# Chained partial sums in two PSUM banks for the seven-product FFN pairs of an encoder layer

## The chip, the cores and the metric

One Trainium2 chip, one core of it. Times are microseconds of device time for one execution of the whole layer. TensorE (PE) multiplies matrices from SBUF into PSUM, VectorE (DVE) and ScalarE (ACT) work on tiles in SBUF and PSUM, GpSimd (POOL) does little here, and SyncE (SP) issues the DMAs. Each engine runs its own instructions in the order in which they were put into its queue when the program was built.

## The reference

One layer over x of 512 tokens by 1024 channels, all in float32:

```
x = LN1(alpha*x + 0.5 * (silu(x @ wg1) * (x @ wu1)) @ wd1)      # FFN 1, inner width 2816
h = x @ w_in ; sparse attention (8 heads) and a short gated convolution on parts of h
x = LN2(alpha*x + concat(attention, convolution) @ w_out)
x = LN3(alpha*x + 0.5 * (silu(x @ wg2) * (x @ wu2)) @ wd2)      # FFN 2, inner width 2816
x = x + sigmoid(x @ w_gate) * (p @ w_proj)
```

The change touches the two products x @ wg and x @ wu of both FFNs and nothing else.

## The kernel before

Every float32 operand of a matmul is split into a high and a low part (`split`, L110: an ACT cast writes the high part, a DVE subtraction the low one), and each product is made of three passes, high x high, high x low, low x high (`PASSES`, L59).

An FFN (`ffn`, L239) goes over 22 chunks of 128 inner channels in five groups of 4, 4, 4, 4 and 6. The first two chunks of an FFN are computed plainly (`plain`). The others go in pairs (`two`, L302): ten pairs in each FFN, twenty in all. A pair computes, for wg and for wu, a 256-channel by 1024 by 512-token product as two by two by two blocks with seven block products instead of eight (Strassen's scheme in Winograd's form). The token side (`Quarters`) keeps the four blocks B11, B21, B22 and the sums T1 to T4; the weight side (`weights`, L269) loads the two row blocks `r` (two DMAs from L274 for each matrix), and makes A11, A12, A22 and the sums S1 to S4, each split into high and low. One product (`prod`, L312) of the pair fills one PSUM bank of 128 x 512: 12 matmuls of 256 columns for wg in one half, 12 for wu in the other half.

After the seven products the partial sums are put together in SBUF (L333 to L342): one copy on ACT and seven additions on DVE, each of which reads one PSUM bank. P5 = S1T1 is read twice. `put_chunk` then makes silu(gate) * up of one 128-channel chunk (L329 on ACT, L330 on DVE) and splits it. The end of each group is the down-projection with wd, matmuls of 512 columns that are accumulated over the group's chunks. In the groups of four these go chunk by chunk with four banks; in the last group they go token block by token block, and each needs all six chunks.

PSUM has eight banks, which `bank("all")` hands out in turn. SBUF tiles are 38 pages of 4 KB per partition in a first-in first-out list (`page`, `free`, L86 to L94). `free` only says in program order which page the next `page` takes; at run time the new owner waits until the last instruction on the old tile is done. A pair before takes 26 pages beside the two of its hidden chunks, gives back raw blocks and plain sums inside `weights`, and everything else (L344) after its second chunk. The loads of a new pair go into such pages too, so a load on SP waits for its page, and later loads wait behind it.

The order on each engine is made by a planner when the program is built. It goes through the program in simulated time; of the instructions that are ready there it takes the one earliest in the program. `tc.high_priority(offset=n)` moves a block n positions ahead in this order. A pair's weight work has a head start of 25 positions (the first pair of FFN 1), 100 (the others of FFN 1), 400 (the first pair of FFN 2) or 50 (the others of FFN 2); the weight rows of the down-projection have 125 in FFN 1 and 0 in FFN 2. A product of a pair is 24 positions long. `WSTEPS` (L31) sets in which turns the two generators of `weights` are pulled.

Of the kernel before, what the change touches and what calls it, by code (L numbers as in the profile page):

```python
# [7 lines left out]
F32 = mybir.dt.float32  # L8
# [4 lines left out]
P = 128  # L13
# [14 lines left out]
REPL = -3.0e38  # L28

NPAGES = 38  # L30
WSTEPS = (1, 2, 1)  # L31
BANKS = ((0, 1), (4, 5), (6,), (7, 2, 3))
AHEAD = 25
AHEAD_N = 150
# [24 lines left out]
PASSES = ((0, 0), (0, 1), (1, 0))  # L59
# [4 lines left out]
def layer_kernel(ctx: ExitStack, tc: tile.TileContext, x, ln1_g, ln1_b, ffn1_wg, ffn1_wu, ffn1_wd, w_in,  # L64
# [21 lines left out]
    def page(shape, dt=F32R):  # L86
        i = free_pages.pop(0)
        t = sb.tile(shape, dt, tag=f"pg{i}", name=f"pg{i}_{count('pg')}")
        owner[id(t)] = (i, t)
        return t  # L90

    def free(*tiles):
        for t in tiles:
            free_pages.append(owner.pop(id(t))[0])  # L94
# [4 lines left out]
    def bank(group):  # L99
        g = GROUPS[group]  # L100
        return pp.tile([P, 512], F32, tag=f"bk{g[count('bank' + group) % len(g)]}", name=f"bk_{count('bank')}")
# [8 lines left out]
    def split(hi, lo, src):  # L110
        nc.scalar.copy(hi, src)  # L111
        nc.vector.tensor_sub(lo, src, hi.bitcast(F32))  # L112
# [126 lines left out]
    def ffn(X, wg, wu, wd, ln_g, ln_b, first, load_nat, groups, nplain, ahead, ahead_f, ahead_d):  # L239
# [26 lines left out]
            nc.vector.tensor_mul(hf, s_t, ps["u"])  # L266
            return put(hf)

        def weights(w, fc, ops, pages):  # L269

            r = []
            for c in (0, 4):
                r.append(page([P, 4, 2 * P], F32))
                nc.sync.dma_start(r[-1], rows(w[:, fc * P:(fc + 2) * P], c * P, 4))  # L274
            A11, A21, A12, A22 = (r[k][:, :, m * P:(m + 1) * P] for k in range(2) for m in range(2))
            a11 = page([P, 2, 4, P])
            split(a11[:, 0], a11[:, 1], A11)
            ops["A11"] = a11[:, 0], a11[:, 1]
            yield
            a2 = page([P, 4, 2 * P]), page([P, 4, 2 * P])  # L280
            split(*a2, r[1])
            ops["A12"], ops["A22"] = (tuple(z[:, :, m * P:(m + 1) * P] for z in a2) for m in range(2))
            yield
            s12, s34 = page([P, 2, 4, P], F32), page([P, 2, 4, P], F32)
            S1, S2, S3, S4 = s12[:, 0], s12[:, 1], s34[:, 0], s34[:, 1]
            nc.vector.tensor_add(S1, A21, A22)  # L286
            nc.vector.tensor_sub(S2, S1, A11)  # L287
            h12 = page([P, 2, 4, P]), page([P, 2, 4, P])
            split(*h12, s12)
            ops["S1"], ops["S2"] = (tuple(z[:, i] for z in h12) for i in range(2))  # L290
            yield
            nc.vector.tensor_sub(S3, A11, A21)  # L292
            nc.vector.tensor_sub(S4, A12, S2)  # L293
            free(*r, s12)
            h34 = page([P, 2, 4, P]), page([P, 2, 4, P])
            split(*h34, s34)
            free(s34)
            ops["S3"], ops["S4"] = (tuple(z[:, i] for z in h34) for i in range(2))
            pages += [a11, *a2, *h12, *h34]
            yield  # L300

        def two(fc, ah):  # L302

            W, pages = {nm: {} for nm, _ in mats}, []
            steps = [weights(w, fc, W[nm], pages) for nm, w in mats]
            with tc.high_priority(offset=ah):
                for n in WSTEPS:
                    for g in steps:
                        for _ in range(n):
                            next(g)  # L310

            def prod(a, b):  # L312

                ps = bank("all").rearrange("p (m n) -> p m n", m=2)
                for i, (nm, _) in enumerate(mats):
                    mm(ps[:, i], [((W[nm][a][0][:, c], W[nm][a][1][:, c]), (X.q[b][0][:, c], X.q[b][1][:, c])) for c in range(4)])
                return ps


            e = [page([P, 2, 2, 256], F32) for _ in range(2)]  # L320
            k = [page([P, 2, 2, 256], F32) for _ in range(2)]
            p1, u2, u3, u4 = k[0][:, 0], k[0][:, 1], k[1][:, 0], k[1][:, 1]
            h = []

            def put_chunk(m):
                hf = ring("hf", 2, [P, 512])
                h3 = hf.rearrange("p (a b) -> p a b", a=2)
                s_t = ring("a", 2, [P, 2, 256])
                nc.scalar.activation(s_t, e[m][:, :, 0], AF.Silu)  # L329
                nc.vector.tensor_mul(h3, s_t, e[m][:, :, 1])  # L330
                h.append(put(hf))

            nc.scalar.copy(p1, prod("A11", "B11"))  # L333
            nc.vector.tensor_add(e[0][:, 0], prod("A12", "B21"), p1)
            nc.vector.tensor_add(u2, prod("S2", "T2"), p1)
            p5 = prod("S1", "T1")
            nc.vector.tensor_add(u4, p5, u2)
            nc.vector.tensor_add(e[0][:, 1], prod("S4", "B22"), u4)  # L338
            put_chunk(0)
            nc.vector.tensor_add(u3, prod("S3", "T3"), u2)  # L340
            nc.vector.tensor_add(e[1][:, 1], p5, u3)
            nc.vector.tensor_add(e[1][:, 0], prod("A22", "T4"), u3)  # L342
            put_chunk(1)
            free(*pages, *e, *k)  # L344
            return h

        f0 = 0
# [449 lines left out]
```

## Time and profile before

| | |
|---|---|
| median of 3 runs | 1026.12 us (1024.97 to 1027.34) |
| profiled execution | 1026.09 us |
| its span, first to last instruction | 1024.0 us |
| mean granted TensorE clock | 0.998 of full speed |
| TensorE, VectorE, ScalarE busy | 98%, 80%, 43% of the span |

All rows below come from the profiled execution. Its time has 2.1 us around the span. Busy time of TensorE counts a matmul from its start to a modelled end, so neighbours overlap; the distance of two starts tells the rate.

### The profile page before, as it was taken

The numbers are of one execution on the slowest core, as the hardware profiler recorded it, in microseconds if no ns is written. First come the engines' busy times: TensorE is split into PE (matmuls) and PEld (weight loads), VectorE is DVE, ScalarE is ACT, GpSimd is POOL, SyncE is SP. The second block draws the span as 40 slices with busy tenths as digits, with TensorE's granted clock in tenths as the row PEclk, the third lists the DMA queues.
The fourth block names the chain that finished last, engine by engine and source line by source line (L and its number), as shares of the span: only waits on it lengthen the run. The fifth ranks groups of instructions, "written<-read, shape, count | busy, mean of one in ns | idle before, by whom it ended". The sixth has DMA issues, their size and how long they took to land.

```text
span 1024.0 us, 15507 instructions
## 1 busy us (share of the span) xinstructions
PE 1004.6 (98%) x6313; PEld 903.8 (88%) x6313; DVE 822.2 (80%) x1283; ACT 441.8 (43%) x621; POOL 25.0 (2%) x35
## 2 busy tenths in 40 slices
PE   8999999999999999999999999999999999999998
PEld 7989999898998878888878778989999898998787
DVE  7897868978697958999479988896868969689852
ACT  6444424433354235332576836443425324246221
POOL 1000000000000200000000011000000000000100
PEclk9999999999999999999999999999999999999999
DMA  9342324323335231424013223331424322227111
GB/s 311 122 123 83 109 98 131 97 83 107 100 119 185 69 92 42 128 58 124 20 42 104 83 65 101 124 124 39 127 83 144 103 79 87 83 85 265 52 41 51
DMA packets 99510, 104.57 MB, mean 102 GB/s; under 512 B 5872, under 2 KB 81904, under 8 KB 99440
## 3 DMA queue, kind: packets, MB, share of 16 engines
q1 hardware_dynamic: 99440, 103.60, 31.8%
q8 instruction: 49, 0.80, 0.3%
q14 instruction: 21, 0.17, 0.1%
HBM read 101.49 MB, written 2.10 MB: 101 GB/s over the span
## 4 chain that ended last, share of the span: by engine, by line
PE 89%; DMA 4%; DVE 3%; ACT 3%; issue 1%; POOLq 0%; SPq 0%; ACTq 0%
PE bk L132 86%; ACT pg L111 2%; DVE pg L112 1%; DMA pg<-in_ffn_wu_dram 1%; PE bk L506 1%; DMA pg<-in_w_in_dram 1%; DMA pg<-in_x_t_dram 1%; PE bk L507 1%; PE bk L704 1%; DMA pg<-in_ple_proj_w_dram 1%; DMA pg<-in_ffn_wd_dram 0%; PE bk L146 0%; ACT a L676 0%; DMA pg<-in_ple_gate_w_dram 0%; PE bk L692 0%
## 5 line engine op out<-in xcount | busy, mean ns | idle before, releaser
L132 PE MATMUL bk<-pg,pg 128*128 128x256 f32 (+1 forms) x2832 | 496.4, 333 | 4.4 <-ACT pg L111 1.8
L132 PEld LDWEIGHTS bk<-pg,pg 128*128 128x128 f32 x2832 | 427.6, 190 | 56.0 <-ACT pg L111 2.6
L111 ACT CAST pg<-pg 128x1024 fp32r<-128x1024 f32 (+1 forms) x267 | 260.0, 984 | 313.3 <-PE bk L132 78.4
L112 DVE TENSOR_TENSOR pg<-pg,pg 128x1024 fp32r<-128x1024 f32 (+1 forms) x267 | 300.6, 1139 | 40.6 <-ACT pg L111 35.5
L132 PE MATMUL bk<-xq,pg 128*128 128x256 f32 x2208 | 275.3, 284 | 4.6 <-DVE mv L158 1.5
L132 PEld LDWEIGHTS bk<-xq,pg 128*128 128x128 f32 x2208 | 270.6, 193 | 7.0 <-ACT pg L111 2.3
L132 PE MATMUL bk<-xT,pg 128*128 128x512 f32 (+2 forms) x600 | 133.0, 381 | 0.3 <-ACT xT L111 0.2
L132 PEld LDWEIGHTS bk<-xT,pg 128*128 128x128 f32 (+1 forms) x600 | 109.9, 186 | 21.5 <-ACT xT L111 0.5
L132 PE MATMUL bk<-pg,xT 128*128 128x512 f32 (+1 forms) x312 | 69.5, 374 | 1.3 <-DVE nat L385 1.3
L132 PEld LDWEIGHTS bk<-pg,xT 128*128 128x128 f32 x312 | 55.0, 188 | 11.4 <-ACT pg L111 1.8
L329 ACT ACTIVATE a<-pg 128x512 f32<-128x512 f32 x40 | 25.2, 629 | 71.7 <-DVE pg L338 66.1
L111 ACT CAST pg<-hf 128x512 fp32r<-128x512 f32 (+1 forms) x56 | 34.6, 618 | 35.2 <-DVE hf L330 19.6
L112 DVE TENSOR_TENSOR pg<-hf,pg 128x512 fp32r<-128x512 f32 (+1 forms) x56 | 38.3, 684 | 4.7 <-ACT pg L111 4.5
L399 DVE SCALAR_TENSOR_TENSOR nat<-bk,nat 128x512 f32<-128x512 f32 x64 | 40.4, 682 | 0.8 <-PE bk L132 0.7
L330 DVE TENSOR_TENSOR hf<-a,pg 128x512 f32<-128x512 f32 x40 | 27.5, 688 | 13.6 <-ACT a L329 13.5
L338 DVE TENSOR_TENSOR pg<-bk,pg 128x512 f32<-128x512 f32 x20 | 13.8, 692 | 29.9 <-PE bk L132 29.4
L160 POOL TENSOR_TENSOR mv<-mv,mhalf 128x1 f32<-128x1 f32 x12 | 17.8, 1480 | 627.0 <-DVE mv L159 627.0
L286 DVE TENSOR_TENSOR pg<-pg,pg 128x512 f32<-128x512 f32 x40 | 27.3, 686 | 5.7 <-DMA pg<-in_ffn_wg_dram 5.7
L292 DVE TENSOR_TENSOR pg<-pg 128x512 f32<-128x512 f32 x40 | 27.4, 686 | 2.9 <-PE bk L132 2.9
L112 DVE TENSOR_TENSOR pg<-bk,pg 128x512 fp32r<-128x512 f32 (+2 forms) x37 | 22.5, 626 | 8.5 <-ACT pg L111 8.1
L287 DVE TENSOR_TENSOR pg<-pg,pg 128x512 f32<-128x512 f32 x40 | 27.3, 685 | 0.0
L293 DVE TENSOR_TENSOR pg<-pg,pg 128x512 f32<-128x512 f32 x40 | 27.1, 686 | 0.1
(100 smaller groups left out, 612.7 us busy)
## 6 DMA issues: line engine op xcount, KB each, us to landing
pg<-in_ffn_wg_dram SPq DMA_DIRECT2D x44, 512.0 KB, 4.1
pg<-in_ffn_wu_dram SPq DMA_DIRECT2D x44, 512.0 KB, 4.7
pg<-in_ffn_wd_dram SPq DMA_DIRECT2D x44, 512.0 KB, 4.0
pg<-in_w_in_dram SPq DMA_DIRECT2D x28, 512.0 KB, 3.6
pg<-in_w_out_dram SPq DMA_DIRECT2D x8, 512.0 KB, 3.9
pg<-in_ple_gate_w_dram SPq DMA_DIRECT2D x8, 512.0 KB, 4.8
pg<-in_x_t_dram SPq DMA_DIRECT2D x4, 512.0 KB, 7.5
nat<-in_x_dram SPq DMA_DIRECT2D x4, 512.0 KB, 8.9
```

Source lines behind the costliest of these rows:

```text
L111: nc.scalar.copy(hi, src)
L112: nc.vector.tensor_sub(lo, src, hi.bitcast(F32))
L132: nc.tensor.matmul(ps, lhsT=st[a], rhs=mv[b], start=first and i == 0 and k == 0, stop=last and i == n - 1 and k == 2)
L160: nc.gpsimd.tensor_tensor(mv[:, 3:4], mv[:, 2:3], mhalf, op=ALU.pow)
L286: nc.vector.tensor_add(S1, A21, A22)
L287: nc.vector.tensor_sub(S2, S1, A11)
L292: nc.vector.tensor_sub(S3, A11, A21)
L293: nc.vector.tensor_sub(S4, A12, S2)
L329: nc.scalar.activation(s_t, e[m][:, :, 0], AF.Silu)
L330: nc.vector.tensor_mul(h3, s_t, e[m][:, :, 1])
L338: nc.vector.tensor_add(e[0][:, 1], prod("S4", "B22"), u4)
L399: nc.vector.scalar_tensor_tensor(dst, acc[t], CY, dst, op0=ALU.mult, op1=ALU.add)
```

## The change

The seven products are computed in the order A11B11, S1T1, S2T2, S4B22, S3T3, A12B21, A22T4. Two PSUM banks, x and y, are each used for several of them, and later products add to what stands there: x holds A11B11, then A11B11 + S2T2, then that plus S3T3, then that plus A22T4; y holds S1T1, then S1T1 + S4B22. A12B21 has a third bank. Between two products the running sum is copied out by ACT (four copies in all) or added by DVE to what is already in the page (three additions). Only the first matmul on a bank has `start` set.

In `weights` the split of the second row block (A12, A22) is the last step instead of the second, S4 is computed before S3, and the two matrices are pulled in turn, one step each. The pages of an operand go back to the list after the product that uses it last, the pages of the sums `e` after their chunk, and the two pages `k` are gone. The hidden chunk m = 0 follows A12B21, the sixth product; before, it followed the fifth.

```diff
--- before.py
+++ after.py
@@ -28,7 +28,6 @@
 REPL = -3.0e38
 
 NPAGES = 38
-WSTEPS = (1, 2, 1)
 BANKS = ((0, 1), (4, 5), (6,), (7, 2, 3))
 AHEAD = 25
 AHEAD_N = 150
@@ -266,7 +265,8 @@
             nc.vector.tensor_mul(hf, s_t, ps["u"])
             return put(hf)
 
-        def weights(w, fc, ops, pages):
+        def weights(w, fc, ops):
+
 
             r = []
             for c in (0, 4):
@@ -275,11 +275,7 @@
             A11, A21, A12, A22 = (r[k][:, :, m * P:(m + 1) * P] for k in range(2) for m in range(2))
             a11 = page([P, 2, 4, P])
             split(a11[:, 0], a11[:, 1], A11)
-            ops["A11"] = a11[:, 0], a11[:, 1]
-            yield
-            a2 = page([P, 4, 2 * P]), page([P, 4, 2 * P])
-            split(*a2, r[1])
-            ops["A12"], ops["A22"] = (tuple(z[:, :, m * P:(m + 1) * P] for z in a2) for m in range(2))
+            ops["A11"] = (a11[:, 0], a11[:, 1]), [a11]
             yield
             s12, s34 = page([P, 2, 4, P], F32), page([P, 2, 4, P], F32)
             S1, S2, S3, S4 = s12[:, 0], s12[:, 1], s34[:, 0], s34[:, 1]
@@ -288,38 +284,51 @@
             h12 = page([P, 2, 4, P]), page([P, 2, 4, P])
             split(*h12, s12)
             ops["S1"], ops["S2"] = (tuple(z[:, i] for z in h12) for i in range(2))
-            yield
+            ops["S1"], ops["S2"] = (ops["S1"], []), (ops["S2"], h12)
+            yield
+            nc.vector.tensor_sub(S4, A12, S2)
             nc.vector.tensor_sub(S3, A11, A21)
-            nc.vector.tensor_sub(S4, A12, S2)
-            free(*r, s12)
+            free(r[0], s12)
             h34 = page([P, 2, 4, P]), page([P, 2, 4, P])
             split(*h34, s34)
             free(s34)
             ops["S3"], ops["S4"] = (tuple(z[:, i] for z in h34) for i in range(2))
-            pages += [a11, *a2, *h12, *h34]
+            ops["S3"], ops["S4"] = (ops["S3"], h34), (ops["S4"], [])
+            yield
+            a2 = page([P, 4, 2 * P]), page([P, 4, 2 * P])
+            split(*a2, r[1])
+            free(r[1])
+            ops["A12"], ops["A22"] = (tuple(z[:, :, m * P:(m + 1) * P] for z in a2) for m in range(2))
+            ops["A12"], ops["A22"] = (ops["A12"], []), (ops["A22"], a2)
             yield
 
         def two(fc, ah):
 
-            W, pages = {nm: {} for nm, _ in mats}, []
-            steps = [weights(w, fc, W[nm], pages) for nm, w in mats]
+            W = {nm: {} for nm, _ in mats}
+            steps = [weights(w, fc, W[nm]) for nm, w in mats]
             with tc.high_priority(offset=ah):
-                for n in WSTEPS:
+                for _ in range(4):
                     for g in steps:
-                        for _ in range(n):
-                            next(g)
-
-            def prod(a, b):
-
-                ps = bank("all").rearrange("p (m n) -> p m n", m=2)
+                        next(g)
+
+            def bank2():
+                return bank("all").rearrange("p (m n) -> p m n", m=2)
+
+            def product(ps, a, b, first):
+
                 for i, (nm, _) in enumerate(mats):
-                    mm(ps[:, i], [((W[nm][a][0][:, c], W[nm][a][1][:, c]), (X.q[b][0][:, c], X.q[b][1][:, c])) for c in range(4)])
+                    w = W[nm][a][0]
+                    for c in range(4):
+                        for k, (x_, y_) in enumerate(PASSES):
+                            nc.tensor.matmul(ps[:, i], lhsT=w[x_][:, c], rhs=X.q[b][y_][:, c],
+                                             start=first and i == 0 and c == 0 and k == 0,
+                                             stop=i == 1 and c == 3 and k == 2, skip_group_check=not first)
+                for nm, _ in mats:
+                    free(*W[nm][a][1])
                 return ps
 
 
             e = [page([P, 2, 2, 256], F32) for _ in range(2)]
-            k = [page([P, 2, 2, 256], F32) for _ in range(2)]
-            p1, u2, u3, u4 = k[0][:, 0], k[0][:, 1], k[1][:, 0], k[1][:, 1]
             h = []
 
             def put_chunk(m):
@@ -328,20 +337,20 @@
                 s_t = ring("a", 2, [P, 2, 256])
                 nc.scalar.activation(s_t, e[m][:, :, 0], AF.Silu)
                 nc.vector.tensor_mul(h3, s_t, e[m][:, :, 1])
+                free(e[m])
                 h.append(put(hf))
 
-            nc.scalar.copy(p1, prod("A11", "B11"))
-            nc.vector.tensor_add(e[0][:, 0], prod("A12", "B21"), p1)
-            nc.vector.tensor_add(u2, prod("S2", "T2"), p1)
-            p5 = prod("S1", "T1")
-            nc.vector.tensor_add(u4, p5, u2)
-            nc.vector.tensor_add(e[0][:, 1], prod("S4", "B22"), u4)
+
+            x_, y_ = bank2(), bank2()
+            nc.scalar.copy(e[0][:, 0], product(x_, "A11", "B11", True))
+            nc.scalar.copy(e[1][:, 1], product(y_, "S1", "T1", True))
+            nc.scalar.copy(e[0][:, 1], product(x_, "S2", "T2", False))
+            nc.vector.tensor_add(e[0][:, 1], product(y_, "S4", "B22", False), e[0][:, 1])
+            nc.vector.tensor_add(e[1][:, 1], product(x_, "S3", "T3", False), e[1][:, 1])
+            nc.vector.tensor_add(e[0][:, 0], product(bank2(), "A12", "B21", True), e[0][:, 0])
             put_chunk(0)
-            nc.vector.tensor_add(u3, prod("S3", "T3"), u2)
-            nc.vector.tensor_add(e[1][:, 1], p5, u3)
-            nc.vector.tensor_add(e[1][:, 0], prod("A22", "T4"), u3)
+            nc.scalar.copy(e[1][:, 0], product(x_, "A22", "T4", False))
             put_chunk(1)
-            free(*pages, *e, *k)
             return h
 
         f0 = 0
```

## Rows read from the trace of the kernel before

**Rows 1.** page, part 1: engines, busy us (share of span) xinstructions
```profile
PE 1004.6 (98%) x6313; PEld 903.8 (88%) x6313; DVE 822.2 (80%) x1283; ACT 441.8 (43%) x621; POOL 25.0 (2%) x35
```

**Rows 2.** chain that ended last, in order: start us, us, what
```profile
11.04 308.99 PE bk L132 x2219
...
629.88 305.84 PE bk L132 x2201
```

**Rows 3.** windows: stretch, us, busy us (x) of PE, PEld, DVE, ACT, POOL, PEclk, DMA, GB/s
```profile
11.00:320.00 309.00, 308.96 (x2220) 293.90 (x2221) 254.69 (x331) 133.36 (x161) 0.00 (x0) 0.99 0.38 120
...
320.00:332.00 12.00, 10.97 (x59) 8.93 (x59) 10.93 (x14) 7.28 (x9) 1.39 (x2) 1.00 0.64 216
...
632.00:935.00 303.00, 303.00 (x2185) 287.94 (x2185) 246.90 (x326) 127.63 (x156) 0.00 (x0) 1.00 0.34 110
```

**Rows 4.** groups by line and shape: busy us, mean ns | idle before
```profile
L333 ACT COPY pg<-bk 128x512 f32<-128x512 f32 x20 | 11.7, 586 | 14.7 <-PE bk L132 14.6
...
L334 DVE TENSOR_TENSOR pg<-bk,pg 128x512 f32<-128x512 f32 x20 | 13.7, 686 | 3.9 <-PE bk L132 3.9
...
L342 DVE TENSOR_TENSOR pg<-bk,pg 128x512 f32<-128x512 f32 x20 | 13.7, 683 | 0.0
...
L111 ACT CAST pg<-pg 128x1024 fp32r<-128x1024 f32 x226 | 235.8, 1050 | 270.3 <-PE bk L132 63.4 <-DVE pg L287 56.4 <-DMA pg<-in_ffn_wd_dram 47.3
...
L112 DVE TENSOR_TENSOR pg<-pg,pg 128x1024 fp32r<-128x1024 f32 x226 | 273.5, 1221 | 37.7 <-ACT pg L111 33.0 <-ACT a L329 2.7 <-PE bk L132 1.7
```

**Rows 5.** timeline: start us, us, instruction; first pair of the third group, FFN 1
```profile
130.19 3.09 SPq L274 DMA_DIRECT2D pg<-in_ffn_wg_dram  x2
...
138.16 5.92 PE L132 MATMUL bk<-xq,pg 128*128 128x256 f32 x48
...
141.23 0.59 ACT L333 COPY pg<-bk 128x512 f32<-128x512 f32 x1 [0.39 <-PE bk L132]
...
152.55 5.92 PE L132 MATMUL bk<-pg,pg 128*128 128x256 f32 x48
...
152.75 0.69 DVE L338 TENSOR_TENSOR pg<-bk,pg 128x512 f32<-128x512 f32 x1 [2.19 <-PE bk L132]
...
158.31 1.96 PE L132 MATMUL bk<-xq,pg 128*128 128x256 f32 x15
...
158.75 0.68 DVE L340 TENSOR_TENSOR pg<-bk,pg 128x512 f32<-128x512 f32 x1
```

**Rows 6.** timeline of the first pair, FFN 1
```profile
37.64 2.01 ACT L111 CAST pg<-pg 128x1024 fp32r<-128x1024 f32 x2 [0.96 <-DMA pg<-in_ffn_wd_dram]
...
39.87 3.04 PE L132 MATMUL bk<-pg,pg 128*128 128x256 f32 x24
...
41.51 0.59 ACT L333 COPY pg<-bk 128x512 f32<-128x512 f32 x1
```

**Rows 7.** timeline of the middle pair of the last group, FFN 1 and FFN 2
```profile
299.79 3.04 PE L132 MATMUL bk<-pg,pg 128*128 128x256 f32 x24
...
300.25 5.77 DVE L112 TENSOR_TENSOR pg<-pg,pg 128x1024 fp32r<-128x1024 f32 x5
...
306.54 0.68 DVE L340 TENSOR_TENSOR pg<-bk,pg 128x512 f32<-128x512 f32 x1
...
911.18 5.92 PE L132 MATMUL bk<-pg,pg 128*128 128x256 f32 x48
...
919.19 0.69 DVE L340 TENSOR_TENSOR pg<-bk,pg 128x512 f32<-128x512 f32 x1
```

**Rows 8.** timeline at the ends of the last pairs, FFN 1 and FFN 2
```profile
325.33 2.58 ACT L111 CAST pg<-pg 128x1024 fp32r<-128x1024 f32 x3 [1.76 <-DMA pg<-in_w_in_dram]
...
327.81 0.63 ACT L329 ACTIVATE a<-pg 128x512 f32<-128x512 f32 x1
...
329.94 2.40 PE L132 MATMUL bk<-pg,pg 128*128 128x512 f32 x8 [1.02 <-ACT pg L111]
...
941.69 4.62 PE L132 MATMUL bk<-pg,pg 128*128 128x512 f32 x19 [0.74 <-ACT pg L111]
```

## The prediction

> **What bounds the kernel now.** I read the engines' busy times first, then the chain of waits, then the two FFN stretches by windows, then the order of single instructions in them. TensorE is busy in 98% of the span, VectorE (DVE) in 80%, ScalarE (ACT) in 43% [rows 1]. The chain that ended last is TensorE without a break for 308.99 us of the first FFN and 305.84 us of the second [rows 2]; all the code that is changed runs in these two pieces. By windows TensorE has 308.96 us of work in 309.00 us and 303.00 in 303.00, at the full granted clock, 0.99 and 1.00 of 2.4 GHz [rows 3]. So no product of a pair waits for anything, and neither do the down-projections between pairs. Two products, 48 matmuls, begin at 152.55, and the next work follows at 158.31, 5.76 us later [rows 5]: one product of 24 matmuls takes 2.88 us, a pair's seven take 20.16. Twenty pairs are 403 us, and the change leaves every matmul in place (seven products of 24 in both kernels). What it can win is only what TensorE loses at the ends of these stretches, and what it can lose is the unbroken stream.
>
> **Evacuations: less VectorE, more ScalarE.** A pair had one ACT copy out of PSUM and seven DVE adds; it gets four copies and three adds. Four adds of 0.68 to 0.69 us go (13.7 or 13.8 us for 20 of each), three copies of 0.586 us come [rows 4]: over 20 pairs DVE loses 80 x 0.688 = 55 us (822 to 767) and ACT gains 60 x 0.586 = 35 us (442 to 477). Both lie beside a TensorE that waits for neither, so the term itself is 0. If that cover were gone, the most that a lighter DVE could give back is what TensorE waits at the two tails, 1.02 + 0.74 = 1.76 us [rows 8].
>
> **The two chained banks: a new wait.** Before, seven products of a pair went to seven banks in turn, and a late evacuation delayed nobody. Now four products of a pair begin only when their own bank has been read: S2T2 after the copy of A11B11, S4B22 after the copy of S1T1, S3T3 after the copy of S2T2's sum (these three on ACT), A22T4 after the DVE add that takes S3T3's sum. In each case exactly one other product, 2.88 us, lies between. Queued behind a waiting product on TensorE is everything: the rest of the pair, the next pair or the down-projection, and so the end. The wait is free while lag + duration stays under 2.88 us, that is up to a lag of 2.3 us for a copy and 2.2 for an add; every microsecond above that is one on the span.
>
> The lags of the nearest instructions before, from the end of the product to the start of its evacuation: mostly 0.2 us (the copy at 141.23 behind a product that ended at 138.16 + 2.88 = 141.04; the add at 152.75 behind one that ended at 152.55) [rows 5]. But the tail is long. S3T3 ended at 155.43 and its add came at 158.75: 3.32 us late, behind DVE's work on the next pair's weights and on the hidden chunk; of such rows one stands here; the first FFN has four, in the first pair of each of its later groups [rows 5]. In the middle pair of the last group it was 306.54 - 299.79 = 6.75 us, with five subtractions of splits in a row ahead of it, and in the second FFN 919.19 - 914.06 = 5.13 us [rows 7]. The first pair's copy came at 41.51 for a product that ended at 39.87 - 2.88 = 36.99: 4.52 us, behind casts in ACT's queue, some of which wait for a load [rows 6]. If all of these stayed under the new order, they would cost 4 x (3.32 + 0.68 - 2.88) = 4.5, 6.75 + 0.68 - 2.88 = 4.6, 5.13 + 0.69 - 2.88 = 2.9 and 4.52 + 0.59 - 2.88 = 2.2 us, together 14.2 us. That is the upper end; the lower end is 0, since a wait can't make the stream shorter.
>
> Which end is nearer? The adds are late because of what stands in DVE's queue ahead of them, and the change thins that out: the hidden chunk's multiply and split (two of some 0.69 us, as the adds on tiles of that size in rows 4) now follow A12B21, one product later, so 3.32 falls to about 2.0, below the limit, at no cost. In the group of three pairs each pair also loses 2.75 us of DVE work, so 6.75 and 5.13 fall to about 2.6 and 1.0 (6.75 - 1.4 - 2.75): 0.4 us and nothing. For the first pair, the split of the second row block, ahead of the sums before, now stands last, which lets the casts ahead of the copy go earlier; half of 2.2 us is left. One further microsecond I add for places that I can't see, since the two copies on S1T1 and S2T2 have no counterpart of their own. Term: 0.4 + 1.1 + 1.0 = +2.5 us, between 0 and 14.2. The planner can also fill a wait that it foresees with A12B21, which has a bank of its own, or with the next pair; I take 1 us off for it: **+1.5 us**.
>
> On this the Trainium skill speaks against the change: Perfetto Trace Analysis, in Optimizing Tensor Performance, Matmuls, has independent groups rotate through different PSUM banks so that an evacuation overlaps the next group's matmuls. The trace before agrees, since lags of 3 to 7 us cost TensorE nothing there. By that rule the sum would go to the upper end, the first rival below.
>
> **Operands and order.** S1, T1 are needed one product after the pair's start rather than three, S4 and S3 each one earlier, S2 where it was, A12 four later. The second row block's split, one cast of 1.05 and one subtraction of 1.22 us for each matrix [rows 4], moves behind the sums and their splits, so S1 and S2 are ready 2 x 1.22 us of DVE time earlier, against the 5.76 us by which S1 is wanted earlier. The rest has to come from the pages: no product waits for a weight now [rows 3], but by the page queue some of a pair's sums get their pages only with the end of the pair before. With pages back after the third and the fifth product they are made sooner, and I put the step at 0; where it stays tight (the last pair of a group of three) a miss would cost at most one product, 2.9 us, once in each FFN (+5.8). The loads' own order on SP's queue is unchanged, but the pages that they wait for change. For the second pair of a group the first raw blocks got pages of hidden chunks that free early in the down-projection's second half, so that a load left at 130.19 [rows 5]; by the page queue it now takes pages of the last weight rows, which free when the pair before begins, 8 us later. Its DVE work then runs beside the first pair, before 158.31: 0, but it crowds DVE where the add ahead of A22T4 falls. Other loads start sooner; no product waits for a load, so this too is 0. Ends: -1.8 us (both tails) to +5.8.
>
> **Tails.** After the last pair the down-projection needs all hidden chunks at once. TensorE waits 1.02 and 0.74 us there. In the first FFN the SiLU of the last chunk came at 327.81, held by three casts on ACT, the first of which had waited for a load [rows 8]. The copy of the last quarter now goes to ACT, into that same queue and ahead of the SiLU: +0.59 us where ACT is the late one. In the second FFN I take it to be the same. Against this stands the lighter DVE. I take +0.3 us each, **+0.6** (ends -1.8 and +1.2).
>
> **Sum.** The profiled execution took 1026.09 us, 1024.0 of it the span and 2.1 around it; the median shown is 1026.12. 1026.1 + 1.5 + 0.6 = 1028.2; the page effects, which have more room below zero than I gave them in the tails, take 0.5 off: **1027.7 us**, 0.15% above. About 0.2%, 2 us, is what a measurement of this kernel tells from no change.
>
> **Rivals.** (1) Slower: the new wait on the bank decides. The planner puts weight work ahead of a gating evacuation, since weights carry a head start of 100 positions in the first FFN and 50 in the second. Price between a third and all of the 14.2 us: 1031 to 1040, more likely near its lower end, 1032. For it: the lags of 3 to 7 us. Against it: VectorE has 55 us less to do, and most lags are 0.2. It decides from a lag of 2.2 us on. (2) Faster: the ends give way. The lighter DVE and the early pages take away both tail waits and something at the start of the second FFN: -1.8 to -4 us, 1022 to 1024. For it: the page queue reaches further ahead. Against: the tails hang on ACT. (3) The clock falls, since gaps at the chained products pull it to its lower level. In this trace the granted clock stayed at 1.00 in the stretch from 320 to 332 us, where TensorE was idle for 1.03 us [rows 3]. One pair at 1.2 instead of 2.4 GHz would cost about its 20.16 us again: 1046. The Trainium skill has this case in TensorE: Matmul & The Clock Gate, A second HAM failure mode: psum-queue depth-cycling: short idle times between groups of matmuls, as banks are cycled, let the clock swing. No stretch of the trace before shows it. (4) The chain is not felt at all, because the planner reorders the products around every wait: 1026, inside the forecast.
>
> **Chances.** Forecast with (4) 0.45 (own range 1025 to 1030), (1) 0.33, (2) 0.20, (3) 0.02. Slower by over 0.2%: 0.30 of (1), 0.07 of the forecast's upper side, 0.02: 0.39. Faster: 0.19 + 0.02 = 0.21. Within: the rest, 0.40. The range that leaves out 0.2: 1022.5 to 1036.
>
> **What would show it.** Right: DVE near 767 us and ACT near 477; both FFN windows still within 2 us of solid TensorE; the add after S3T3 at a lag under 2.2 us in nearly all pairs. Wrong on the chain: TensorE idle before L132 products named to an ACT copy or to the DVE add, several us in sum, most in the first FFN. Wrong on the tails: the waits at the two down-projections gone or doubled. The prediction fails as a whole if the time moves by more than 2 us either way, and in its mechanism if that happens outside the FFN stretches.

## The result: 0.56% slower, and the profile after

The changed kernel takes 1032.28 us (median of 6 runs, 1030.20 to 1035.43), the kernel before 1027.01 us (6 runs, 1024.97 to 1029.42); the ratio is 1.0056, 95% interval 1.0036 to 1.0075. The profiled span is 1030.6 us, against 1024.0 before. This is the page's first part, busy us, share of the span and instructions of each engine, the counterpart of [rows 1]:

```profile
PE 1005.8 (98%) x6313; PEld 902.3 (88%) x6313; DVE 782.6 (76%) x1203; ACT 472.1 (46%) x681; POOL 25.5 (2%) x35
```

The edit is there: 80 DVE instructions fewer, 60 ACT instructions more, the same 6313 matmuls. TensorE's work is 1.2 us longer and its span 6.6 us longer, so it waits, and the question is where. From 30 us on the granted clock is 1.00 in every stretch. I cut both executions into stretches that end at the same points of the program: with the last product of the first FFN's pairs, the last transposes of its layer norm, a point 12 us into the second FFN, its last product and its last transposes. These windows have other cuts than [rows 3]. The first fence is the kernel before, the second the one after; columns are the stretch, its length, TensorE's busy us (matmuls), clock, DMA share and GB/s.

```profile
30.00:322.83 292.83, 292.83 (x2100) 1.00 0.34 110
322.83:368.00 45.17, 42.79 (x202) 1.00 0.36 108
368.00:632.00 264.00, 257.19 (x1261) 1.00 0.24 72
632.00:937.10 305.10, 305.10 (x2203) 1.00 0.34 110
937.10:982.50 45.40, 43.74 (x208) 1.00 0.27 96
982.50:1024.00 41.50, 37.47 (x189) 1.00 0.14 51
```

```profile
30.00:321.56 291.56, 291.56 (x2087) 1.00 0.35 112
321.56:369.80 48.24, 43.42 (x202) 1.00 0.29 83
369.80:634.00 264.20, 257.10 (x1260) 1.00 0.24 71
634.00:940.70 306.70, 305.52 (x2204) 1.00 0.35 112
940.70:989.10 48.40, 44.08 (x208) 1.00 0.22 76
989.10:1030.60 41.50, 37.43 (x189) 1.00 0.14 51
```

Row by row. Pairs of the first FFN: they end 1.27 us earlier, but 13 matmuls fewer were left at 30 us. The 49th matmul (without the six on the tile `warm` at the very start) begins at 15.31 us, before at 16.83. The reason is not the change but the granted clock: in the profile of the kernel before it stood at its lower level, 1.2 GHz, from 11.14 to 14.55 us, and 17 matmuls ran where the changed kernel ran 29 at 2.4 GHz (the same window, first before, then after):

```profile
11.14:14.55 3.41, 3.41 (x17) 0.50 1.18 307
11.14:14.55 3.41, 3.41 (x29) 1.00 1.18 307
```

From the 49th matmul on the same work takes 1.52 - 1.27 = 0.25 us longer. First tail (the last down-projection with its layer norm): 48.24 against 45.17, **+3.07 us** for the same 202 matmuls. The middle: +0.20. Pairs of the second FFN: 306.70 against 305.10, +1.60. Second tail: 48.40 against 45.40, **+3.00** for the same 208 matmuls. The rest: 0.00. Together -1.5 + 0.25 + 3.07 + 0.20 + 1.60 + 3.00 = 6.6 us, the difference of the spans. Of the 8.1 us that are lost behind the start, 6.07, three quarters, fall into the two tails, which hold none of the change's products.

What TensorE waits for in the tails is on the list of its waits, which sums them by waiting and releasing line (us in total, times, longest). Of the kernel after:

```profile
PE bk L145 <- DVE nat L161: 6.0, 7, 2.1
...
PE bk L323 <- DVE pg L349: 1.2, 1, 1.2
```

Of the kernel before, the same first wait (its lines are one higher):

```profile
PE bk L146 <- DVE nat L162: 0.9, 2, 0.6
```

L145 is the transposition of a finished token block, L161 the last step of that block's layer norm. That wait has grown from 0.9 to 6.0 us, and all of it lies in the two tails: some 5 of their 6.07 us. The wait that the prediction feared, a chained product (L323) behind its evacuation, happens once, for 1.18 us. The timeline shows both; columns are start, duration, instruction, and the idle time before it with its releaser. First the first block of the first tail, after the change:

```profile
327.14 0.96 PE L131 MATMUL bk<-pg,pg 128*128 128x512 f32 x3 [1.08 <-ACT pg L110]
...
328.48 8.72 PE L131 MATMUL bk<-pg,pg 128*128 128x512 f32 x37 [0.38 <-DVE pg L111]
...
332.76 1.21 DVE L111 TENSOR_TENSOR pg<-pg,pg 128x1024 fp32r<-128x1024 f32 x1
333.88 0.69 DVE L394 SCALAR_TENSOR_TENSOR nat<-bk,nat 128x512 f32<-128x512 f32 x1
...
335.81 1.54 POOL L159 TENSOR_TENSOR mv<-mv,mhalf 128x1 f32<-128x1 f32 x1 [6.04 <-DVE mv L158]
337.38 1.28 DVE L161 SCALAR_TENSOR_TENSOR nat<-nat,mv,pg 128x1024 f32<-128x1024 f32 x1 [0.46 <-POOL mv L159]
...
338.72 1.09 PE L145 MATMUL bk<-ident,nat 128*128 128x128 f32 x8 [1.52 <-DVE nat L161]
```

In the program's order the transposes stand 23 matmuls behind the block's last one. TensorE was through with those at 338.72 - 1.52 = 337.20, and at some 0.23 us each (8.72 us for 37) the block itself had ended near 331.9. From L394, which takes its second half out of PSUM, to the end of L161 it is 333.88 to 338.66, 4.8 us, a chain through DVE, POOL and DVE again; and L394 began 2 us late, behind a weight split. 23 matmuls cover 5.3 us of the 6.8, and 1.5 are left as a wait. Then the end of the second FFN's last pair, and its first block:

```profile
933.37 1.05 ACT L110 CAST pg<-pg 128x1024 fp32r<-128x1024 f32 x1 [4.84 <-DMA pg<-in_ffn_wd_dram]
...
935.84 1.23 DVE L111 TENSOR_TENSOR pg<-pg,pg 128x1024 fp32r<-128x1024 f32 x1 [0.17 <-ACT pg L110]
936.98 0.68 DVE L349 TENSOR_TENSOR pg<-bk,pg 128x512 f32<-128x512 f32 x1
...
937.72 3.14 PE L323 MATMUL bk<-pg,pg 128*128 128x256 f32 x24 [1.18 <-DVE pg L349]
...
945.09 9.41 PE L131 MATMUL bk<-pg,pg 128*128 128x512 f32 x40 [0.52 <-ACT pg L110]
...
956.60 1.09 PE L145 MATMUL bk<-ident,nat 128*128 128x128 f32 x8 [2.10 <-DVE nat L161]
```

The bank's add L349 (after S3T3) stood behind a subtraction of a wd split, whose cast had waited 4.84 us for a load: the mechanism of the first rival, once. In the kernel before, the transposes of the first block in the first tail did not wait at all:

```profile
329.94 10.36 PE L132 MATMUL bk<-pg,pg 128*128 128x512 f32 x43 [1.02 <-ACT pg L111]
...
338.50 1.27 DVE L162 SCALAR_TENSOR_TENSOR nat<-nat,mv,pg 128x1024 f32<-128x1024 f32 x1
...
340.14 1.03 PE L146 MATMUL bk<-ident,nat 128*128 128x128 f32 x8
```

The margin was small: the layer norm (L162) was done at 339.77, 0.37 us before the transposes. It took no less time than in the changed kernel; what differs is the cover. That can be counted in the two programs, as TensorE's queue was written when they were built: matmuls between a token block's last one and its transposes.

```
                       FFN 1, blocks 0 to 3     FFN 2, blocks 0 to 3
before                 33  36  26  24           33  28  24  29
after                  23  20  24  24           20  20  24  29
after, late transposes 36  36  25  24           36  36  28  30
chain only             31  30  25  24           27  21  24  29
pages only             30  28  24  24           20  23  24  29
```

By its rule the planner puts the transposes where its simulated time has the layer norm done; that time itself is not on record. In the changed kernel the layer norm on the chip is done later than its transposes stand in the queue, and TensorE, which runs its queue in order, stops there. The changed kernel got the shorter distances for blocks 0 and 1, both in tails whose own code is unchanged.

### The profile page after: what moved, and what is told of

Same layout as the page of the kernel before. It is cut to its first block, busy times and chain, and to the rows that moved or that the text cites. A ratio compares the mean times of both kernels' runs of the same rounds, so it can differ in the third digit from the quotient of the medians.

```text
span 1030.6 us, 15433 instructions
## 1 busy us (share of the span) xinstructions
PE 1005.8 (98%) x6313; PEld 902.3 (88%) x6313; DVE 782.6 (76%) x1203; ACT 472.1 (46%) x681; POOL 25.5 (2%) x35
## 4 chain that ended last, share of the span: by engine, by line
PE 86%; DVE 5%; DMA 4%; ACT 2%; issue 1%; POOL 1%; POOLq 0%; SPq 0%; ACTq 0%; DVEq 0%
PE bk L131 44%; PE bk L323 38%; DVE pg L111 1%; ACT pg L110 1%; DMA pg<-in_ple_gate_w_dram 1%; PE bk L515 1%; DMA pg<-in_ffn_wu_dram 1%; DVE nat L161 1%; PE bk L145 1%; PE bk L516 1%; DMA pg<-in_ffn_wd_dram 1%; DMA pg<-in_x_t_dram 1%; PE bk L713 1%; POOL mv L159 1%; DMA pg<-in_ple_proj_w_dram 1%
## 5 line engine op out<-in xcount | busy, mean ns | idle before, releaser
L111 DVE TENSOR_TENSOR pg<-pg,pg 128x1024 fp32r<-128x1024 f32 (+1 forms) x267 | 299.1, 1139 | 97.1 <-ACT pg L110 83.5
L131 PE MATMUL bk<-pg,pg 128*128 128x512 f32 (+1 forms) x1392 | 318.7, 384 | 5.0 <-DVE nat L748 2.0
L323 PE MATMUL bk<-xq,pg 128*128 128x256 f32 x1920 | 240.1, 283 | 0.0
L323 PEld LDWEIGHTS bk<-xq,pg 128*128 128x128 f32 x1920 | 235.2, 192 | 0.6
L323 PE MATMUL bk<-pg,pg 128*128 128x256 f32 x1440 | 182.9, 283 | 1.2 <-DVE pg L349 1.2
L323 PEld LDWEIGHTS bk<-pg,pg 128*128 128x128 f32 x1440 | 177.1, 192 | 1.6 <-DVE pg L349 1.4
L111 DVE TENSOR_TENSOR pg<-hf,pg 128x512 fp32r<-128x512 f32 (+1 forms) x56 | 38.3, 685 | 7.0 <-ACT pg L110 6.8
L159 POOL TENSOR_TENSOR mv<-mv,mhalf 128x1 f32<-128x1 f32 x12 | 17.8, 1480 | 639.2 <-DVE mv L158 639.2
L111 DVE TENSOR_TENSOR pg<-bk,pg 128x512 fp32r<-128x512 f32 (+2 forms) x37 | 22.5, 626 | 8.2 <-ACT pg L110 7.8
```

The source lines that it names most:

```text
L131: nc.tensor.matmul(ps, lhsT=st[a], rhs=mv[b], start=first and i == 0 and k == 0, stop=last and i == n - 1 and k == 2)
L159: nc.gpsimd.tensor_tensor(mv[:, 3:4], mv[:, 2:3], mhalf, op=ALU.pow)
L323: nc.tensor.matmul(ps[:, i], lhsT=w[x_][:, c], rhs=X.q[b][y_][:, c], start=first and i == 0 and c == 0 and k == 0, stop=i == 1 and c == 3 ...
```

## The experiments

Two theories at first. **Tail**: the loss is the transposes, placed too close behind their block. **Chain**: the loss comes from the banks that are shared, through late evacuations or what they push back. All times below are beside the kernel before on the same chip, 1026.49 us (33 runs) for the first four, 1026.59 (15) for the last four.

**The changed kernel with its transposes later**, everything else as it is; the first block's are issued after the second's matmuls, the second's after the third's:

```diff
-                    transpose_tb(yT, t, "all")
+                    for k in ((), (0,), (1, 2), (3,))[t]:
+                        transpose_tb(yT, k, "all")
```

> The changed kernel with one edit outside the change: in the last down-projection of each FFN the transposes of token block 0 are emitted after block 1 and those of block 1 after block 2, so that 36 matmuls instead of 20 to 23 stand between a block's end and its transposes. Tail theory (the loss is TensorE waiting at these transposes for the layer norm): the waits of 1.68, 0.50, 2.26 and 0.49 us go, 1032.3 - 4.9 = 1027.4 us. Chain theory (the loss is the wait on the chained banks, spread over the pairs): no change, 1031.5 to 1032.5.

1026.24 us (12 runs), ratio to before 0.999 (0.9972 to 1.0008), against 1.0056 for the change as it was. The tails are back to the length they had before, 45.51 and 44.92 us (TensorE windows):

```profile
321.79:367.30 45.51, 42.77 (x202) 1.00 0.31 87
...
937.68:982.60 44.92, 43.62 (x209) 1.00 0.25 82
```

and the waits show what is left of the chain, 0.6 + 0.5 us in both FFNs together, the transposes at 0.8:

```profile
PE bk L145 <- DVE nat L161: 0.8, 1, 0.8
...
PE bk L323 <- DVE pg L349: 0.6, 1, 0.6
PE bk L323 <- ACT pg L347: 0.5, 2, 0.3
```

The layer norm of the first tail's first block runs as in the changed kernel, step for step, and ends at 338.89 us against 338.67; only the transposes come later, at 340.20, and find it done. One edit outside the pairs takes 6.0 us back, as the tail theory has it. The next run shows how much of this the edit gives to the kernel before as well.

**The kernel before with the same edit.**

> The kernel before with the same edit of the transposes. Tail theory: its blocks 0 and 1 wait nothing at their transposes (28 to 36 matmuls stand between), so no change, within 0.7 us of before. If the edit gains by something else than those waits, it gains here too, 3 us or more.

1024.72 us (12 runs), 0.9979 (0.9961 to 0.9997): 1.8 us less than the kernel before, between the two expectations, and the fastest of all versions. The gain can't be placed. In its profile the two tails are not shorter, 46.07 and 45.70 us (45.17 and 45.40 before), and the span is 1.5 us shorter because of the start, where the clock was 1.00 here and not in the earlier profile:

```profile
30.00:321.03 291.03, 291.03 (x2086) 1.00 0.35 111
321.03:367.10 46.07, 42.96 (x202) 1.00 0.36 106
...
935.60:981.30 45.70, 43.79 (x209) 1.00 0.28 96
```

So not all of the 6.0 us was the change's loss. With late transposes in both kernels the change costs 1026.24 - 1024.72 = 1.5 us, which the scatter of 12 runs each hardly tells from nothing; without them it costs 1032.28 - 1027.01 = 5.3. So about three quarters of the loss go with the place of the transposes; by the windows, too, three quarters lie in the tails.

**The chained banks alone**: the evacuations and the order of products of the change, with the weight steps and the pages of before.

```diff
-            nc.scalar.copy(p1, prod("A11", "B11"))
-            nc.vector.tensor_add(e[0][:, 0], prod("A12", "B21"), p1)
...
+            nc.scalar.copy(e[0][:, 0], product(x_, "A11", "B11", True))
+            nc.scalar.copy(e[1][:, 1], product(y_, "S1", "T1", True))
+            nc.scalar.copy(e[0][:, 1], product(x_, "S2", "T2", False))
...
```

> The kernel before with the chained banks, the new evacuations and the new order of products alone; weight steps and pages as before. Chain theory: the whole loss, +5 us, 1032. Tail theory: in the built program 31, 30, 25, 24 matmuls (FFN 1) and 27, 21, 24, 29 (FFN 2) stand between a block and its transposes; the waits of the changed kernel show that about 30, 22, 25 and 30, 22, 27, 33 are wanted; that leaves about 2.6 us of waits against 1.3 in the kernel before: +1.3, 1028.3 us.

1032.55 us (12 runs), 1.005 (1.0032 to 1.0067). Nearer to the chain theory's number, yet for another reason: of the waits few are on a bank (0.3 + 0.3), 1.8 us on weights (L112, L111), most of them at the first pair of the second FFN, and 2.3 on transposes (0.9 before). The profile is of an execution of 1030.55 us, its shortest, and these waits are only 3.8 us more than in the kernel before; the rest of the 6.1 is not placed:

```profile
PE bk L146 <- DVE nat L162: 2.3, 4, 1.1
...
PE bk L320 <- DVE pg L112: 1.2, 2, 0.8
...
PE bk L320 <- ACT pg L111: 0.6, 1, 0.6
```

**The weight steps and the pages alone**: the products, banks and evacuations of before, the second row block split last, operands given back with their last product.

```diff
-WSTEPS = (1, 2, 1)
...
-            free(*r, s12)
+            free(r[0], s12)
...
-            free(*pages, *e, *k)
+            free(*k)
```

> The kernel before with the new weight steps and the early return of pages alone; products, banks and evacuations as before. Chain theory: no change, 1027. Tail theory: 30, 28, 24, 24 and 20, 23, 24, 29 matmuls stand between: about 3.7 us of waits against 1.3, so +2.4, 1029.4 us.

1033.73 us (10 runs), 1.0065 (1.0043 to 1.0087). Again slower than expected, and by other waits: 7.1 us in four on an ACT cast. The timeline has three of them at the down-projections after the last pairs (328 and 950 us), where the last hidden chunk comes late, and in the first pairs of the second FFN (663 us):

```profile
328.31 4.01 PE L131 MATMUL bk<-pg,pg 128*128 128x512 f32 x11 [2.14 <-ACT pg L110]
...
662.64 5.42 PE L131 MATMUL bk<-xq,pg 128*128 128x256 f32 x43 [1.68 <-ACT pg L110]
...
949.82 14.39 PE L131 MATMUL bk<-pg,pg 128*128 128x512 f32 x55 [2.58 <-ACT pg L110]
```

Here the clock has a part, as it has not in the changed kernel's profile. Soon after the first and the last of these waits it stood at 0.50 for 3.4 us (the second from 951.19 to 954.60), with 9 matmuls in a stretch where 15 would fit at 0.23 us each:

```profile
329.96:333.38 3.42, 3.42 (x9) 0.50 0.55 154
```

So each half costs 6 to 7 us, and both together no more than that.

**The DVE additions put back as idle work.** Is it the lighter VectorE that makes the planner place the transposes early? Four additions per pair, into a tile that nobody reads, in the changed kernel:

```diff
+            spare(e[0][:, 0])
+            spare(e[1][:, 1])
             nc.vector.tensor_add(e[0][:, 1], product(y_, "S4", "B22", False), e[0][:, 1])
+            spare(e[0][:, 1])
...
+            spare(e[1][:, 0])
             put_chunk(1)
```

> The changed kernel with four additions of 128x512 on VectorE put back into every pair, into a tile that nobody reads, so that VectorE has as much to do as before. Theory A (the transposes come too early because VectorE became lighter): the loss goes, 1027 us. Theory B (what counts is which splits stand in VectorE's queue at the tail, and these hang on the pages): in the built program still 24, 20 and 20, 20 matmuls stand before the first two transposes, so the loss stays, 1031 to 1033 us.

1035.21 us (5 runs), 1.0085 (1.007 to 1.0101). The waits at the transposes stay (5.6 us), so that idea falls. The three microseconds on top are partly the chain's: its waits on a DVE add are 2.3 us now, where the change had 1.2. In this profile the clock also stood at 0.50 from 960.30 to 963.71 us, soon after a wait of 1.93 us at a transpose.

```profile
PE bk L145 <- DVE nat L161: 5.6, 7, 1.9
...
PE bk L323 <- DVE pg L355: 2.3, 3, 1.0
```

**The chain alone, with late transposes.** Now the transposes are out of the way, and what the chain costs without its weight steps shows.

> Chained banks, evacuations and order of products alone (weight steps and pages as before), with the transposes moved as in e1. What is left against the kernel before with the same transposes (0.998 of before) is the chain's own wait. The trace of the chain alone showed 2.5 us of TensorE's waits in the pairs: 1027.0 us. If the chain were free: 1024.5.

1031.58 us (5 runs), 1.0053 (1.0038 to 1.0068). Both expectations missed. At the first pair of the second FFN a product waits for weights, 2.1 us in two steps, and the clock stands at 0.50 from 664.04 to 667.45 us: the next 24 matmuls take 4.24 us instead of 3.04.

```profile
661.86 0.50 PE L320 MATMUL bk<-xq,pg 128*128 128x256 f32 x2 [1.30 <-ACT pg L111]
...
663.12 1.77 PE L320 MATMUL bk<-xq,pg 128*128 128x256 f32 x10 [0.76 <-DVE pg L112]
...
664.69 4.24 PE L320 MATMUL bk<-pg,pg 128*128 128x256 f32 x24
```

**The pages alone, with late transposes.**

> Early return of pages and new weight steps alone, with the transposes moved as in e1 (block 0 of the second FFN still has 20 matmuls in the built program). No chain. Tail theory: of the 7 us of loss without the move about half goes (the waits at the transposes, 2.0 us, and some behind them): 1029 to 1031. If the early pages were the whole loss by themselves, 1033 stays.

1030.20 us (10 runs), 1.0042 (1.0021 to 1.0063), in the expected range. The casts' waits are still there, in the profile of an execution of 1035.25 us; the ten runs go from 1028.20 to 1036.08, and the four with a mean clock of 0.999 or more take 1030.18 at most. In the profile the clock stood at 0.50 from 661.71 to 665.12 and from 948.43 to 955.26 us, around the waits of 1.81 us at 660.45 and 2.63 us at 949.26.

```profile
PE bk L131 <- ACT pg L110: 7.5, 4, 2.7
```

With late transposes, then, the chain alone stands at +0.53%, the pages alone at +0.42%, both together at -0.10%, and the kernel before at -0.21%. A part of the halves' loss is the clock: over all their runs the mean granted clock was 0.9966 (chain, late) and 0.9975 (pages, late), against 0.9988 in the kernel before with late transposes. As an estimate, that share of some 1030 us is 2.3 and 1.3 us of their 6.9 and 5.5. Products in the order A11B11, S1T1, S2T2, S4B22, S3T3, A12B21, A22T4 want S1 to S4 early and A12 late; the old weight steps split A12 second, the new ones last. Either half alone asks for weights in an order in which they aren't made. That this is why the two halves don't add is argued from where the waits lie; no run separates it from the pages.

**Nothing between the chained products.** With late transposes, the changed kernel in the order A11B11, S2T2 (bank x), S1T1, S4B22 (y), A12B21, S3T3, A22T4 (x): three of the four gated products come directly after the product whose sum must leave the bank.

```diff
-            nc.scalar.copy(e[1][:, 1], product(y_, "S1", "T1", True))
             nc.scalar.copy(e[0][:, 1], product(x_, "S2", "T2", False))
+            nc.scalar.copy(e[1][:, 1], product(y_, "S1", "T1", True))
...
-            nc.vector.tensor_add(e[1][:, 1], product(x_, "S3", "T3", False), e[1][:, 1])
             nc.vector.tensor_add(e[0][:, 0], product(bank2(), "A12", "B21", True), e[0][:, 0])
+            nc.vector.tensor_add(e[1][:, 1], product(x_, "S3", "T3", False), e[1][:, 1])
```

> The changed kernel with the transposes moved as in e1, and the products in an order in which three of the four chained products of a pair follow directly on the product whose sum must first be read: A11B11, S2T2 on x, S1T1, S4B22 on y, A12B21, S3T3, A22T4 on x. If nothing hides the wait, each of the 60 costs 0.2 + 0.59 + 0.1 = 0.9 us: +54 us, 1080. If the planner fills it with matmuls of the next product, as the built program shows (6 to 11 matmuls of another bank, 0.72 to 1.3 us), only about 0.2 us are left at 20 of them and up to 0.9 at the ten last products without a filler: +4 to +13, 1030 to 1039. If the wait is no cost at all: 1026.

1047.04 us (4 runs), 1.0205 (1.019 to 1.022), between the expectations: 20.8 us over the same kernel with one product between (1026.24). So the bank's turn has a price, and the 2.88 us of a product between hide nearly all of it. That it is not more is likely the planner's doing, which by the expectation's count had put 6 to 11 matmuls of another bank into the gaps; no run takes them out. In the trace the price has two halves. Some 9.5 us are waits:

```profile
PE bk L323 <- ACT pg L347: 7.7, 9, 1.5
...
PE bk L323 <- DVE pg L350: 1.8, 2, 1.4
```

The other half is in steps too short for this list: two L323 matmuls begin 0.12 us apart, but at 94 places here 0.15 to 0.42 us, 10.1 us more together; the changed kernel has 5 such places, 0.5 us.

## Why the prediction was right in its range and wrong in its place

**Sum.** 1027.7 was forecast as the likeliest, with 1031 to 1040 at 0.33 for the first rival; measured is 1032.28. The time is the rival's, the cause is not. The forecast's own test speaks against it: the time moved by more than 2 us, mostly outside the pairs. That it lies inside the stated range is luck: what brought it there, 6.07 us in the tails, stands in no term.

**Tails: the step that failed.** The term was +0.6 us with ends -1.8 and +1.2; the windows show +3.07 and +3.00. I took the waits that the rows of before show, 1.02 and 0.74 us on an ACT cast [rows 8], and asked whether the copy of the last quarter would lengthen them. Those waits hardly moved: 1.08 us on the cast and 0.38 on a subtraction in the first tail, 0.52 on the cast in the second. The loss came in a place where the trace of before shows next to nothing, the transposes: there they went from 0.9 to 6.0 us. TensorE had 33 and 36 matmuls of cover in the first tail for a layer norm of some 5 to 7 us, and I read a missing wait as a safe place. It was cover that the built order gave, with 0.37 us to spare, and the edit changed this order. "Named as a wait of before" is not the list of what can become one. The upper end of +1.2 was too low for the same reason: it bounded the waits that were there, not the cover behind those that weren't.

**The chained banks.** Term +1.5 us between 0 and 14.2. Measured in the change: +0.25 us in the first FFN's pairs and +1.60 in the second's, of which one wait on the add after S3T3 makes 1.18. With late transposes 1.1 us of such waits are left. The kind of wait and its place within a pair, S3T3's add behind weight work on DVE [rows 7], were right, and so was the sign that the forecast named: the add's lag is under 2.0 us in 18 of the 20 pairs, 2.23 in one and 3.48 in the last. That the size agrees is in part luck: the forecast had 1.1 us in the first pair of the first FFN, 0.4 in that FFN's last group and nothing at the adds of the second, besides 1.0 for places unseen; the one wait came in the last pair of the second. The direction in VectorE's load was right too: with the four additions put back the waits on that add went from 1.2 to 2.3 us, in one profile each. That a product between is needed is shown by its opposite, 20.8 us.

The Trainium skill advises to let independent groups rotate through PSUM banks (Perfetto Trace Analysis, Optimizing Tensor Performance, Matmuls). The runs agree with it where nothing lies between (+20.8 us), and not in the form that would bring the sum to the upper end, since with 2.88 us of other work between, 1 to 2 us are felt.

**Evacuations.** ACT came to 472.1 us (477 forecast), VectorE to 782.6 (767). VectorE fell by 39.6 us and not by 55. The adds removed are as long as forecast: summed one by one, DVE's instructions went from 898.5 to 845.7 us, 52.8 less. But neighbours on DVE overlap in the records (adds of 0.68 us that follow each other start 0.60 apart, as below, in the kernel with additions put back), and busy time counts an overlap once: the overlaps were 76.3 us before and 63.1 after. It changes nothing for TensorE.

```profile
302.03 0.69 DVE L355 TENSOR_TENSOR pg<-bk,pg 128x512 f32<-128x512 f32 x1
302.63 0.68 DVE L356 TENSOR_TENSOR pg<-bk,pg 128x512 f32<-128x512 f32 x1
```

**Operands and pages.** 0, and that held for the change as a whole: no product of a pair waits on a weight there. It holds for the two edits together only: with the chain alone products of a pair waited 1.8 us for weights in all, with late transposes 2.1, and with the pages alone one waited 1.7 us in the second FFN's first pair. The prediction weighed them apart and didn't ask whether the order of weights has to go with the order of products.

**Rivals.** (2), the ends give way: the opposite happened. (3), the clock: from 30 us on 1.00 in every window of the change, and a mean of 0.999 in the version with 20.8 us more, so idle time at chained products didn't pull it down. It was not as steady as the prediction has it, though. The 0.99 in [rows 3] is the stretch of 3.41 us at 0.50 shown above, and with the pages alone, the pages with late transposes, the chain with late transposes and the additions put back it fell after waits of 1.8 to 2.6 us or two that make 2.1 together, once during such a wait; in the change it stayed at 1.00 after one of 2.10. (4), the planner reorders around waits: by the count in its expectation it does in the version with nothing between; in the tails its order is what made the loss.

**What stays open.** Why the planner foresees a quicker layer norm, or finds fewer matmuls to put ahead of the transposes, in the changed program. Chain alone and pages alone each shorten the distances somewhat, and VectorE's lighter load is not the reason. Open too are the 0.2% that the kernel before gains by late transposes, and the part of the halves' loss that neither waits nor clock account for.

## What to carry to other kernels

When an order is written at build time from simulated durations, list the places where an in-order engine stands behind a long chain on other engines, and how much cover each has in the order as built; then compare that cover between the two programs before looking at the edit. A wait that is absent from a trace may be absent by a margin of less than a microsecond, here 0.37 us. A running sum in one PSUM bank costs little while another product lies between two additions to it and takes longer than the evacuation with its lag; here that was 2.88 us against lags of mostly under 2 us and copies and adds of 0.6 to 0.7.

## What the runs showed that was not expected

A tail of 202 matmuls that no line of the change touches became 3 us longer, and one edit there was worth 6 us (1032.28 to 1026.24), of which the kernel before gains 1.8 too. Two halves of a change that cost 0.5% and 0.65% apart cost 0.56% together, and with the transposes later 0.1% over the kernel before with the same edit. The power on a 128 x 1 tile on GpSimd, one number per partition, takes 1.5 us (1.54 us at L159 above), nearly a third of the 4.8 us from the last read of PSUM to the end of the layer norm. And the start of an execution varies by up to 2.9 us between the ten profiles: the 49th matmul begins between 14.8 and 15.6 us in seven of them, and at 16.0, 16.8 and 17.7 in the three whose clock stood at 0.50 for 3.4, 3.4 and 6.8 us in the first 16 us, with the change and without. So a stretch has to be measured from its own first instruction, beside its granted clock.
